# Moving reads and waits in a one-core hybrid attention step: paired read-backs, splits at the change of token group, other tiles for turned outputs, and x rows by GpSimd

## The chip, the cores and the metric

The kernel runs on one core of a Trainium2 chip. The metric is the device time in microseconds (us) of one execution; the number that counts is the median of the runs. Beside the timed runs there is one profiled execution, from which all views of the profile come.

## What is computed

One layer of a streaming encoder: an input projection, two kinds of attention (stick-breaking and retention, 8 heads each, head width 128), a gate, and an output projection. There are 1024 prompt frames and 128 sample frames (8 streams of 16), and 1024 cached frames for each stream. Cut to what matters here:

```python
h = rms_norm(x, norm_pre)
q_sb, k_sb, v_sb, gate_sb, q_r, k_r, v_r, gate_r = split(h @ w_in)    # 2048 -> 8 x 1024
q_r, k_r = rope(q_r), rope(k_r) * HEAD_DIM ** -0.5

def stick_breaking_block(q, k, v):            # a block of 128 queries, keys up to it
    z = q @ k.T * HEAD_DIM ** -0.5
    log_keep = where(strict, log_sigmoid(-z), 0)
    later = reverse_cumsum(log_keep) - log_keep
    return where(strict, exp(log_sigmoid(z) + later), 0) @ v

def retention_chunk(q, k, v, s, log_gamma):   # 64 frames, a state s of 128 x 128
    o = (q @ k.T * gamma ** abs(i - j)) @ v + (q @ s) * decay_read
    s = s * gamma ** n + (k * decay_write).T @ v
    return o, s

y = concat(head_norm(o_sb) * gain * silu(gate_sb), head_norm(o_r) * gain * silu(gate_r))
x = x + rms_norm(y @ w_out, norm_post)        # w_out: 2048 x 2048
```

New keys, values and the retention states are outputs too.

## The kernel before, in words

**Products.** All large products are in 32-bit floats made of two parts. A *split* takes a block and gives a high part, rounded to the matmul's format, by a copy on ScalarE (ACT), and the rest by a subtraction on VectorE (DVE). Each product is then three matmuls (high by high, high by low, low by high). The matmuls run on TensorE (PE).

**Token groups and heads.** The tokens go in two groups: group 0 is prompt tiles 0 to 3 and the sample tile (640 tokens), group 1 prompt tiles 4 to 7 (512 tokens). x lies in SBUF split, in the tiles mh0 to mh3 (high) and ml0 to ml3 (low), each with four of the 16 blocks of 128 columns. For each group there is a loop over 8 heads. A head has a *rows panel* (`project_rows`, matmul at L451), which gives values and gates of the head with weights as the moving operand, 16 steps of k by the tiles of the group by three matmuls, and *projections* (`project`, `products`, L394) for the retention's keys and queries and the stick-breaking's queries and keys, with x as the moving operand. The last head of group 0 takes two of them side by side (`project_pair`). The results leave PSUM by `rope` (two copies on ACT at L495 and L496, three operations on DVE at L497, L498 and L499) or by a multiplication on DVE (L470). The accumulators have four PSUM banks in two rings, acc0 and acc1; a panel of the next head needs banks that ropes must have read.

**Jobs.** Everything else of a head (attention, outputs, loads for later) is written as generators that are *jobs*. After each product of three matmuls the program calls `tick()`, which lets one due job take a step; the number that a job yields is the number of ticks until it is due again. The tables D_* hold these numbers, in pairs for group 0 and group 1. `drain(job)` ticks without products until a job is done. From this program order a scheduler places the instructions on each engine; `pin` ties an instruction so that it is not placed ahead of the products already written. Each engine then runs its own list in order, and a waiting instruction holds up all behind it. A DMA stands in the list of the engine that issues it: SyncE (SP) for most loads, ACT for most stores, GpSimd (POOL) for some of both.

**Transposes through DRAM.** Rows are turned by a store (`turn_out`, L642), a read-back in 32-blocks (`turn_in`, L651) and a transpose on DVE: L747 for the stick-breaking weights of a step (tiles kb, or kp and be), L874 for those of the sample, L1028 for the retention's keys (into rkn), and L722 for a branch's finished output. In `Out.finish` that transpose (L722) goes into a tile that is free by then, rk for the retention and kT for the stick-breaking, is multiplied by the gains (L723), and is stored to DRAM (s_y) for the output projection. The last attention jobs of group 0 run on in the first head of group 1; rk is then also the tile into which that head's `rope` of the keys goes.

**The start.** The x columns are split as they come, for two projections. Then comes the first rows panel. Its jobs (`squares`, L534 for the load, L542 for the operation on ACT) read the rows of x again, in 18 pieces of 512 KB, for the sums of squares of the pre-norm. The panel's weights wrn are loaded at L442, by the same queue, SP.

**The change of token group.** `load_moving` reads the 16 blocks of x of group 1 (tile mr, three buffers, L264) and splits them (L172, L173) in the order of k: 12 of its steps are taken inside `project_pair`, two ahead of each of the six chunks after the first pair (`WQ // 2 if loads and w else 0`), and four in the first four steps of the first rows panel of group 1.

**The output projection.** It is done with seven products of half-size blocks (1 to 7) in place of eight, with sums of blocks made ahead and held in DRAM (s_s for left operands, s_b for weights). A left operand, 8 blocks of 128 x 256, is read back from s_y or s_s by `left()` and split into resident tiles. It keeps two blocks loaded ahead (three buffers mr in group 0; three ahead and four buffers yr in group 1), and before each split the load of a further block is issued; `left_sample` does the same for the sample tile (128 x 128). There are 14 such operands and two of the sample. Weights come through wr (five buffers) by SP as well (L1219) and are split (L167, L168); the matmuls stand at L1202, L1205 and L1206.

## Time and profile before

| | us |
|---|---|
| runs | 2277.29, 2277.5, 2275.72 |
| median | 2277.29 |
| the profiled execution, its own time | 2273.69 |
| its span, first to last instruction | 2271.9 |
| PE busy | 2225.6 (98%) |
| DVE busy | 1264.8 (56%) |
| ACT busy | 922.7 (41%) |
| POOL busy | 421.7 (19%) |
| mean granted clock of PE | 0.994 |

So 1.8 us lie around the span, and the profiled execution is 3.6 us shorter than the median. A row of the timeline has the start, the duration, the engine, the line and the operation with its output and inputs; in brackets stands how long the engine was idle before it, and what ended that idle time. SPq is the queue of DMA issues on SP: the duration there is the time over which the group was issued, and a long one means that the queue stood in between. In the list of waits a row has the waiting engine and line, what released it, the total in us, how often, and the longest. In the windows the columns are the stretch, its length, the busy time of PE, PEld (weight loads), DVE, ACT and POOL with the number of instructions in brackets, the granted clock of PE as a share of full speed, and the DMA engines' busy share and GB/s.

### The profile page before, as it was taken

Reading aid. Unit: us, or ns where it says so; the run is one execution under the profiler, and the core shown is the slowest. Engines: PE = TensorE matmul, PEld = TensorE weight load, DVE = VectorE, ACT = ScalarE, POOL = GpSimd, SP = SyncE. Lnnn points to the kernel's source line nnn. Section 1 sums busy time; section 2 is a strip of 40 time slices with the busy share of each in tenths; the row PEclk is TensorE's granted clock in tenths of the full one; section 3 lists DMA queues with packets and bytes.
Section 4 is the critical chain, followed back from the end, with each engine's and each line's share of the span. In section 5 each row is a group of like instructions: output and inputs, shape, how many; then the busy total and the mean of one; then the engine's idle time right before and its main releaser. Section 6 shows DMA issues by size and latency. Waiting matters only on the chain.

```text
span 2271.9 us, 34748 instructions
## 1 busy us (share of the span) xinstructions
PE 2225.6 (98%) x12002; PEld 1887.4 (83%) x12002; DVE 1264.8 (56%) x2688; ACT 922.7 (41%) x2000; POOL 421.7 (19%) x706
## 2 busy tenths in 40 slices
PE   8999999999999999999999999999999999999998
PEld 7888889798888979797778888888888787778886
DVE  5335445453544445355556666656666657656667
ACT  6423333333333332334333343443433435545563
POOL 0022131322212231221212111120212113000020
PEclk9999999999999999999999999999999999999999
DMA  8567565576656656667767777888788777765785
GB/s 293 175 193 199 180 190 181 176 197 199 193 182 176 206 174 194 185 187 271 204 171 221 241 231 228 234 235 236 234 243 220 216 215 194 236 217 162 215 224 169
DMA packets 383986, 471.25 MB, mean 207 GB/s; under 512 B 121409, under 2 KB 238657, under 8 KB 383297
## 3 DMA queue, kind: packets, MB, share of 16 engines
q1 hardware_dynamic: 256304, 300.41, 44.5%
q0 software_dynamic: 33840, 86.28, 14.1%
q10 hardware_dynamic: 93664, 82.33, 11.6%
q8 instruction: 94, 1.54, 0.3%
q14 instruction: 84, 0.68, 0.1%
HBM read 367.97 MB, written 110.36 MB: 211 GB/s over the span
## 4 chain that ended last, share of the span: by engine, by line
PE 82%; DMA 7%; issue 4%; DVE 4%; ACT 2%; POOL 0%; SPq 0%; DVEq 0%; ACTq 0%; POOLq 0%
PE accm L451 32%; PE acc L394 26%; PE a L1205 5%; PE a L1206 5%; PE a L1202 5%; PE pa L784 2%; PE z L757 2%; PE pd L885 1%; PE zc L824 1%; DMA ro<-s_rk 1%; DMA s_rk<-rk 1%; DMA mr<-x_cols 1%; ACT wh L167 1%; DMA wr<-w_cols 1%; PE rs L906 1%
## 5 line engine op out<-in xcount | busy, mean ns | idle before, releaser
L451 PE MATMUL accm<-whn,mh 128*128 128x512 f32 x1152 | 453.1, 394 | 5.5 <-DVE rq L497 3.7
L451 PE MATMUL accm<-wln,mh 128*128 128x512 f32 x1152 | 453.3, 394 | 1.9 <-DVE wln L168 1.9
L394 PE MATMUL acc<-mh,wh 128*128 128x256 f32 (+2 forms) x1536 | 444.4, 340 | 10.9 <-ACT wh L167 7.1
L451 PE MATMUL accm<-whn,ml 128*128 128x512 f32 x1152 | 453.6, 394 | 0.0
L394 PE MATMUL acc<-ml,wh 128*128 128x256 f32 (+2 forms) x1536 | 445.8, 341 | 0.0
L394 PE MATMUL acc<-mh,wl 128*128 128x256 f32 (+2 forms) x1536 | 445.4, 341 | 0.0
L167 ACT ACTIVATE wh<-wr 128x512 fp32r<-128x512 f32 x408 | 256.7, 631 | 463.2 <-PE acc L394 201.8
L168 DVE TENSOR_TENSOR wl<-wr,wh 128x512 fp32r<-128x512 f32 x408 | 279.2, 687 | 272.4 <-ACT wh L167 258.7
L168 DVE TENSOR_TENSOR wln<-wrn,whn 128x512 fp32r<-128x512 f32 x256 | 175.1, 688 | 296.2 <-ACT whn L167 289.9
L167 ACT ACTIVATE whn<-wrn 128x512 fp32r<-128x512 f32 x256 | 160.9, 632 | 400.2 <-PE accm L451 260.1
L394 PEld LDWEIGHTS acc<-mh,wh 128*128 128x128 f32 x1536 | 284.5, 189 | 30.3 <-ACT wh L167 7.8
L394 PEld LDWEIGHTS acc<-mh,wl 128*128 128x128 f32 x1536 | 282.3, 189 | 25.4 <-issue 6.2
L394 PEld LDWEIGHTS acc<-ml,wh 128*128 128x128 f32 x1536 | 281.7, 189 | 20.6 <-issue 1.7
L451 PEld LDWEIGHTS accm<-whn,mh 128*128 128x128 f32 x1152 | 217.3, 189 | 50.8 <-DVE rq L497 4.7
L451 PEld LDWEIGHTS accm<-wln,mh 128*128 128x128 f32 x1152 | 217.4, 189 | 46.8 <-DVE wln L168 3.5
L451 PEld LDWEIGHTS accm<-whn,ml 128*128 128x128 f32 x1152 | 217.4, 189 | 43.5 <-issue 0.8
L651 POOL DMA_DIRECT2D be<-s_be x128 | 94.1, 742 | 145.1 <-DMA s_be<-be 121.1
L687 DVE TENSOR_TENSOR_SCAN kp<-kp 128x1152 f32<-128x1152 f32 (+4 forms) x40 | 82.7, 2068 | 55.2 <-POOL kp L682 27.9
L1202 PE MATMUL a<-wh,mh 128*128 128x512 f32 x240 | 94.1, 392 | 1.7 <-ACT mh L1262 1.7
L1205 PE MATMUL a<-wl,mh 128*128 128x512 f32 x240 | 93.7, 390 | 1.0 <-DVE wl L168 1.0
L1206 PE MATMUL a<-wh,ml 128*128 128x512 f32 x240 | 93.9, 391 | 0.0
L809 POOL DMA_DIRECT2D kcT<-cache_k x64 | 34.6, 544 | 298.9 <-PE acc L394 123.8
(283 smaller groups left out, 2964.8 us busy)
## 6 DMA issues: line engine op xcount, KB each, us to landing
wr<-w_cols SPq DMA_DIRECT2D x256, 256.0 KB, 4.4
wrn<-w_rows SPq DMA_DIRECT2D x256, 256.0 KB, 3.7
kcT<-cache_k POOLq DMA_DIRECT2D x64, 512.0 KB, 5.0
vc<-cache_v SPq DMA_DIRECT2D x64, 512.0 KB, 5.3
wr<-s_b SPq DMA_DIRECT2D x80, 256.0 KB, 3.8
wr<-w_out SPq DMA_DIRECT2D x80, 256.0 KB, 3.8
br<-w_out SPq DMA_DIRECT2D x64, 256.0 KB, 4.4
s_b<-br ACTq DMA_DIRECT2D x32, 512.0 KB, 5.4
```

The source lines that it names most:

```text
L167: nc.scalar.activation(hi, src, AF.Copy),
L168: nc.vector.tensor_tensor(lo, src, hi.bitcast(F32), ALU.subtract),
L394: last = nc.tensor.matmul(a[:, :m], lhs[:, j, :], rhs[w][:, j, o : o + m], start=(w == 0 and j == 0 and n == 0), stop=(w == KT // WQ - 1 a ...
L451: anchor[0] = nc.tensor.matmul(banks[t], lhs[q][:, j, ts], rhs, start=(k == 0 and n == 0), stop=(k == KT - 1 and n == 2),)
L651: q.dma_start(raw[32 * i : 32 * i + 32, :].rearrange("p (k a) -> p k a", a=32), s[:, :, 32 * i : 32 * i + 32].rearrange("k (j b) a -> b (k ...
L687: nc.vector.tensor_tensor_scan(rev, rev, rev, 1.0, ALU.mult, ALU.bypass)
L757: nc.tensor.matmul(z[:, :c], q2[a][:, i * P : (i + 1) * P], k2[b][:, s : s + c], start=(m == 0), stop=(m == 2),)
L784: nc.tensor.matmul(po[:, :P], at[:, j, :], rest["vn"][j], start=(j == 0), stop=(j == t))
L809: ld = nc.gpsimd.dma_start(kc, cache_k[h, m // 4, m % 4])
L1202: ins = nc.tensor.matmul(a, hi[k][:, ts], wh, start=first, stop=False)
L1205: nc.tensor.matmul(a, hi[k][:, ts], wl, start=False, stop=False)
L1206: anchor[0] = nc.tensor.matmul(a, lo[k][:, ts], wh, start=False, stop=last)
```

## The change

- The rows of x for the sums of squares (xt) are issued by GpSimd, not SyncE.
- The x splits of group 1: inside `project_pair` the steps per chunk are given by `LOADS = 0, 2, 1, 1` (two columns each, so 8 in all); 8 more stand in the first rows panel, at each k but every fourth. Loads and splits are pinned.
- `Out.finish` of the retention transposes into rkn, not rk; that of the stick-breaking in group 1 into the tile be of step 2, not kT.
- `overlap()` adds `D_LATE = 8` ticks, for jobs of group 0 that run on in group 1, ahead of steps that read turned rows. In group 1 D_RK, the wait between a read-back of the keys and its transpose, goes from 18 to 22 ticks.
- `left()` loads blocks in pairs to a buffer of two, as many pairs as there are buffers (three in mr, two in yr), waits D_LEFT = 18 ticks (9 for operands made by `both`), and then splits; the load of a further pair stands behind the second split of a pair. `left_sample` loads all 8 blocks into two buffers of four, waits 18 or 9 ticks, and splits.

No matmul, split, rope or transpose is added or taken away.

```diff
-D_RK = (36, 18)
+D_LATE = 8
+D_RK = (36, 22)
+LOADS = 0, 2, 1, 1
+D_LEFT = 18
...
+    def overlap():
+        return D_LATE if group[0] > phase[0] else 0
...
         def load(k):
             r = wp.tile([P, n], F32, name="mr", tag="mr", bufs=MR)
-            nc.sync.dma_start(r, src(k))
+            pin(nc.sync.dma_start(r, src(k)))
...
-    def left(gi, n, hi, lo, bufs, tag, deep):
+    def left(gi, n, hi, lo, bufs, tag, deep, wait):
...
-        for h in range(deep - 1):
-            load(h)
-        yield D_OP
+        for pair in range(deep):
+            load(pair)
+        yield wait
         for h in range(HT):
-            if h + deep - 1 < HT:
-                load(h + deep - 1)
-            r = raw.pop(0)
-            pin(*split(hi[h], lo[h], r))
+            pin(*split(hi[h], lo[h], raw.pop(0)))
+            if h % 2 and h // 2 + deep < HT // 2:
+                load(h // 2 + deep)
             yield D_OP
...
-                for _ in range(WQ // 2 if loads and w else 0):
+                for _ in range(LOADS[w] if loads else 0):
                     next(loads, None)
...
-            if loads and q == 0:
+            if loads and k % 4 != 3:
                 next(loads, None)
...
-                    nc.sync.dma_start(xt, x_rows(t)[:, c * HALF : (c + 1) * HALF])
+                    nc.gpsimd.dma_start(xt, x_rows(t)[:, c * HALF : (c + 1) * HALF])
...
-                    yield D_TB[phase[0]]
+                    yield D_TB[phase[0]] + overlap()
...
-                        yield D_TR[phase[0]]
+                        yield D_TR[phase[0]] + overlap()
...
-                yield D_TI[phase[0]] // 2
+                yield D_TI[phase[0]] // 2 + overlap()
...
-            yield from out.finish(1, gi, h, 0, rk, s_y[gi][H + h])
+            yield from out.finish(1, gi, h, 0, rkn.rearrange("p k d -> p (k d)"), s_y[gi][H + h])
...
-            yield from out.finish(0, gi, h, 0, kT, s_y[gi][h][:, :NB_TOK])
+            yield from out.finish(0, gi, h, 0, rows[2][1] if gi else kT, s_y[gi][h][:, :NB_TOK])
...
-                made.append(left(g, n, *mine[g, n], *((rp, "yr", 4) if g else (wp, "mr", MR))))
+                made.append(left(g, n, *mine[g, n], *((rp, "yr", 2) if g else (wp, "mr", MR)), D_LEFT // 2))
...
-        ready = [Job(left_sample(1, *mine["s", 1], fp, "ys", 4), 24)]
+        ready = [Job(left_sample(1, *mine["s", 1], fp, "ys", 2, D_LEFT // 2), 24)]
```

The lines of the changed kernel are a few higher than those of before: L495 to L499 are now L501 to L505, L167 and L168 are L170 and L171, L172 is L176, L722 and L723 are L728 and L729, L747 is L753, L874 is L881, L989 and L1007 are L996 and L1014.

How the instructions stand at three places. First ACT at the change of token group. mh is the high part of x (from mr), whn a weight split of the coming rows panel, and the two accumulators are the retention's queries of the last head of group 0, whose rope begins with sw. Before:

```order
L167 ACTIVATE whn<-wrn 128x512
L172 ACTIVATE mh_10431<-mr,pre 128x512
L167 ACTIVATE whn<-wrn 128x512
L172 ACTIVATE mh_10511<-mr,pre 128x512 x3
L167 ACTIVATE whn<-wrn 128x512
L495 ACTIVATE sw<-acc_10263 64x256
L496 ACTIVATE sw<-acc_10263 64x256
L172 ACTIVATE mh_10511<-mr,pre 128x512
L495 ACTIVATE sw<-acc_10264 64x384
L496 ACTIVATE sw<-acc_10264 64x384
```

And with the change:

```order
L170 ACTIVATE whn<-wrn 128x512
L176 ACTIVATE mh_10431<-mr,pre 128x512
L170 ACTIVATE whn<-wrn 128x512
L176 ACTIVATE mh_10431<-mr,pre 128x512
L170 ACTIVATE whn<-wrn 128x512
L176 ACTIVATE mh_10431<-mr,pre 128x512
L501 ACTIVATE sw<-acc_10263 64x256
L502 ACTIVATE sw<-acc_10263 64x256
L501 ACTIVATE sw<-acc_10264 64x384
L502 ACTIVATE sw<-acc_10264 64x384
```

The splits of the third x tile no longer stand ahead of the ropes and between them: eight x splits in all stand ahead now, where there were eleven, and one between.

Second, DVE in the first head of group 1, where attention of group 0's last head runs on: the transpose of the weights kb of a step, the sample's retention (ro, st) and the rope of the new keys (rk, sw). Before:

```order
L168 TENSOR_TENSOR wl<-wr,wh 128x512
L747 STREAM_TRANSPOSE kb<-kb 128x384
L168 TENSOR_TENSOR wl<-wr,wh 128x512
L989 SCALAR_TENSOR_TENSOR ro<-pa,dec,ro 128x128
L1007 SCALAR_TENSOR_TENSOR st<-st,pSs_11261 128x256
L989 SCALAR_TENSOR_TENSOR ro<-pa,dec,ro 128x128
L1007 SCALAR_TENSOR_TENSOR st<-st,pSs_11262 128x256
L498 TENSOR_TENSOR sw<-sw,sinT 128x512
L1007 SCALAR_TENSOR_TENSOR st<-st,pa 128x256
```

With the change:

```order
L996 SCALAR_TENSOR_TENSOR ro<-pa,dec,ro 128x128
L1014 SCALAR_TENSOR_TENSOR st<-st,pSs_11226 128x256
L996 SCALAR_TENSOR_TENSOR ro<-pa,dec,ro 128x128
L1014 SCALAR_TENSOR_TENSOR st<-st,pSs_11227 128x256
L503 TENSOR_TENSOR rk<-acc_11113,cosT 128x512
L1014 SCALAR_TENSOR_TENSOR st<-st,pa 128x256
L881 STREAM_TRANSPOSE kp<-be 128x1152
L1014 SCALAR_TENSOR_TENSOR st<-st,pSs_11240 128x256
L793 COPY so<-pa 128x128
L187 TENSOR_SCALAR ov<-ssq_10041 128x5
L753 STREAM_TRANSPOSE kb<-kb 128x384
```

The transpose of kb stands behind the sample's retention and behind the first read of the keys' bank, where it stood ahead of both.

Third, DVE some 25 us later: the transpose of the retention's finished output (ro), the same for the sample (do), and the ropes. Before:

```order
L168 TENSOR_TENSOR wl<-wr,wh 128x512 x2
L722 STREAM_TRANSPOSE rk<-ro 128x640
L723 TENSOR_SCALAR ro<-rk,gains 128x640
L497 TENSOR_TENSOR rk<-acc_11120,cosT 128x512
L722 STREAM_TRANSPOSE doT<-do 128x128
L499 TENSOR_TENSOR rk<-rk,sw 128x512
```

With the change:

```order
L171 TENSOR_TENSOR wl<-wr,wh 128x512 x2
L503 TENSOR_TENSOR rq<-acc_11353,cosT 128x512
L504 TENSOR_TENSOR sw<-sw,sinT 128x512
L505 TENSOR_TENSOR rq<-rq,sw 128x512
L728 STREAM_TRANSPOSE rkn<-ro 128x640
L915 TENSOR_TENSOR sc<-rs,dT 128x128
L729 TENSOR_SCALAR ro<-rkn,gains 128x640
```

The keys' rope has left this place (it stands in the piece above, some 40 rows ahead), and the queries' rope now stands ahead of the transpose.

More of the change, by code (lines that the diff above doesn't have):

```diff
@@ L202, in tile_hybrid_step @@
     phase = [0]
+    group = [0]
     anchor = [None]
@@ L316, in sums, with load, left_sample @@
             yield pace[2]
[L318 removed]
+    def left(gi, n, hi, lo, bufs, tag, deep, wait):
         src = LEFT[n]
         raw = []
[L322 to L332 removed]
+        def load(pair):
+            r = bufs.tile([P, 2, 256], F32, name=tag, tag=tag, bufs=deep)
+            for i in range(2):
+                h = 2 * pair + i
+                if src[0] == "y":
+                    rows = s_y[gi][src[1] * H + h][:, src[2] * 256 : src[2] * 256 + 256]
+                else:
+                    rows = s_s[gi][h][:, src[1], :]
+                pin(nc.sync.dma_start(r[:, i], rows))
+                raw.append(r[:, i])
+        for pair in range(deep):
+            load(pair)
+        yield wait
         for h in range(HT):
[L334 to L337 removed]
+            pin(*split(hi[h], lo[h], raw.pop(0)))
+            if h % 2 and h // 2 + deep < HT // 2:
+                load(h // 2 + deep)
             yield D_OP
[L340 removed]
+    def left_sample(kk, hi, lo, bufs, tag, deep, wait):
         raw = []
[L343 to L350 removed]
+        for part in range(2):
+            r = bufs.tile([P, HT // 2, P], F32, name=tag, tag=tag, bufs=deep)
+            for i in range(HT // 2):
+                pin(nc.sync.dma_start(r[:, i], s_y[0][kk * H + part * HT // 2 + i][:, 4 * P : 5 * P]))
+                raw.append(r[:, i])
+        yield wait
         for h in range(HT):
[L352 to L353 removed]
             pin(*split(hi[h], lo[h], raw.pop(0)))
@@ L789, in stick_breaking @@
                 yield D_AV[phase[0]]
+            return rows
         waiting = []
@@ L1046, in sb_branch @@
             yield D_NAT[phase[0]]
-            yield from stick_breaking(g, h, out, q2, k2, rest)
+            rows = yield from stick_breaking(g, h, out, q2, k2, rest)
             store_rows(tiles, values[gi, h][:, :, 0, :], v_prompt, v_sample, h)
@@ L1073, in first_left @@
             mine[0, 5] = kept(0)
-            return left(0, 5, *mine[0, 5], wp, "mr", MR)
+            return left(0, 5, *mine[0, 5], wp, "mr", MR, D_LEFT)
         ret_job = sb_job = sub = loads = None
@@ L1083, in tile_hybrid_step @@
                 load_rope(gi)
-            phase[0] = gi
+            phase[0] = group[0] = gi
             for h in range(H):
@@ L1107, in ret_last @@
                     rest = first_left()
+                    next(rest)
                     ret_queries(project(g, mov, col(4, h), rest))
```

33 lines of the change are left out of this document (9 added, 24 removed).

## The prediction, made before the changed kernel had run

> **What bounds the kernel now.** I read the page's first part, then the list of what PE waited for, then windows cut where the granted clock changes.
>
> ```profile
> span 2271.9 us, 34748 instructions
> PE 2225.6 (98%) x12002; PEld 1887.4 (83%) x12002; DVE 1264.8 (56%) x2688; ACT 922.7 (41%) x2000; POOL 421.7 (19%) x706
> ```
>
> PE is the bound: it idles for 2271.9 - 2225.6 = 46.3 us. The change adds and removes no matmul, so it can gain only out of these 46.3 us, and out of the time in which PE runs at a lower clock. Where the idle time lies:
>
> ```profile
> PE acc L394 <- ACT wh L167: 7.1, 1, 7.1
> PE pa L784 <- DVE kp L747: 6.0, 6, 2.3
> PE accm L451 <- DVE rq L497: 3.7, 2, 2.2
> PE acc L394 <- DVE rk L497: 3.5, 1, 3.5
> PE pSs L1003 <- DVE st L1007: 2.6, 1, 2.6
> PE a L1202 <- ACT wh L167: 2.0, 2, 1.1
> PE a L1205 <- DVE wl L168: 1.7, 4, 1.0
> PE a L1202 <- ACT mh L1262: 1.7, 1, 1.7
> PE accm L451 <- ACT whn L167: 1.6, 1, 1.6
> ```
>
> The first row is the start of the kernel, which nothing here touches. The others are single stalls of 1 to 3.5 us, each with its own place, and most are a wait behind something else on DVE or ACT. The windows show what follows such a stall (the granted clock stands after POOL's busy time):
>
> ```profile
> 64.93:68.34 3.41, 3.31 (x8) 2.66 (x9) 2.08 (x4) 3.23 (x6) 0.00 (x0) 0.50 0.70 219
> 1044.55:1051.38 6.83, 5.04 (x12) 3.65 (x13) 5.17 (x12) 5.21 (x9) 0.00 (x0) 0.50 0.79 241
> 1119.65:1123.06 3.41, 3.41 (x16) 2.81 (x18) 1.85 (x5) 1.64 (x4) 0.00 (x0) 0.50 0.28 92
> 1140.13:1146.96 6.83, 6.01 (x14) 4.84 (x15) 3.15 (x7) 1.82 (x3) 2.75 (x5) 0.50 0.55 172
> 1766.20:1772.00 5.80, 5.61 (x33) 4.96 (x34) 2.42 (x11) 2.41 (x5) 0.00 (x0) 1.00 0.72 221
> 2020.00:2261.65 241.65, 241.65 (x1067) 199.74 (x1065) 155.62 (x327) 123.54 (x281) 19.78 (x23) 1.00 0.66 188
> ```
>
> Four times the clock is 0.50, for 3.41 or 6.83 us. Half of that is lost: 1.7, 3.4, 1.7 and 3.4 us, 10.2 us in all. The fifth row shows a stall (2.33 us, quoted below) with no such loss. The last row shows the output projection's second part without any idle time: 241.65 us for 1067 matmuls, 0.227 us each, which is the pitch of a 512-wide matmul.
>
> The Trainium skill (TensorE: Matmul & The Clock Gate, Part 1: The HAM clock gate) says that the clock is halved after an idle window of some 3.4 us that runs freely, and is restored after as long a busy one. The lengths 3.41 and 6.83 us agree with one window and two. That idle spans of under 3 us were enough here disagrees, if the window must be idle throughout.
>
> **The change part by part.**
>
> *First rows panel.* SP first, the queue of loads:
>
> ```profile
> 27.11 12.00 SPq L442 DMA_DIRECT2D wrn<-w_rows  x6
> 50.84 5.45 SPq L534 DMA_DIRECT2D xt<-x_prompt  x4
> 56.38 1.87 SPq L442 DMA_DIRECT2D wrn<-w_rows  x4
> ```
>
> then ACT and PE:
>
> ```profile
> 63.62 1.97 ACT L167 ACTIVATE whn<-wrn 128x512 fp32r<-128x512 f32 x3 [6.00 <-DMA wrn<-w_rows]
> ```
>
> ```profile
> 64.31 0.49 PE L451 MATMUL accm<-whn,mh 128*128 128x512 f32 x1 [1.63 <-ACT whn L167]
> ```
>
> The x rows xt go ahead of the panel's weights wrn in SP's list, which stands at them until a buffer is free; so weights are issued again only at 56.38, ACT waits 6.00 us for them and PE 1.63, and the clock drops. With xt in POOL's list SP has only weights here. What has to hide the new place: POOL has nothing else to issue at this time (0.00 busy in the window at 64.93), and the only loads behind xt there are the cached keys (kcT), which come with the attention jobs after the panel. ACT's sums of squares still stand between weight splits, and each waits for its xt. Both queues move blocks of this size in the same time (size in KB, then us from issue to landing):
>
> ```profile
> kcT<-cache_k POOLq DMA_DIRECT2D x64, 512.0 KB, 5.0
> xt<-x_prompt SPq DMA_DIRECT2D x16, 512.0 KB, 5.1
> ```
>
> A panel step of five tiles takes 15 x 0.227 = 3.4 us, 16 of them 54 us, against 18 loads in four buffers, 18 / 4 x 5 = 23 us. So it is hidden twice over. Gain: 1.63 + 1.7 = **3.3 us**.
>
> *The change of token group.* ACT, then PE:
>
> ```profile
> 1042.35 0.72 ACT L172 ACTIVATE mh<-mr,pre 128x512 fp32r<-128x512 f32 x1 [1.21 <-DMA mr<-x_cols]
> 1043.61 0.38 ACT L495 ACTIVATE sw<-acc 64x256 f32<-64x256 f32 x1
> ```
>
> ```profile
> 1039.26 0.45 PE L394 MATMUL acc<-mh,wl 128*128 128x256 f32 x2
> 1039.55 0.45 PE L394 MATMUL acc<-mh,wh 128*128 128x256 f32 x2
> ```
>
> ```profile
> 1044.89 0.80 PE L451 MATMUL accm<-whn,mh 128*128 128x512 f32 x1 [2.24 <-DVE rq L497]
> 1047.98 0.79 PE L451 MATMUL accm<-whn,mh 128*128 128x512 f32 x1 [1.45 <-DVE rq L497]
> ```
>
> The ropes of the queries start at 1043.61 because x splits that wait for their DMA stand ahead on ACT. But the queries' accumulators are complete a whole chunk before PE's last product of the pair: 12 products of two pieces at 0.29 us (1039.55 - 1039.26), 3.5 us. With three splits fewer ahead, the ropes can run beside PE's last chunk, and end with it. Bounds: if ACT is still late, only the pieces between the ropes fall, the second wait, 1.45 us; if it is in time, both waits and the clock, 2.24 + 1.45 + 3.4 = 7.1 us. I take **6.0**, near the upper end, since the order has the ropes directly behind a split whose x was due some microseconds sooner. The price is eight x splits of 0.72 us in the panel rather than four; a panel step of four tiles is 12 x 0.227 = 2.7 us there, so they fit beside it.
>
> *Transpose of kb.* DVE, then PE:
>
> ```profile
> 1116.13 0.58 DVE L747 STREAM_TRANSPOSE kb<-kb 128x384 f32<-128x384 f32 x1 [5.03 <-DMA kb<-s_be]
> ```
>
> ```profile
> 1117.92 0.59 PE L1003 MATMUL pSs<-vv,rkn 32*128 32x128 f32 x3 [2.57 <-DVE st L1007]
> ```
>
> DVE stands 5.03 us for a read-back, with the sample's retention and the keys' rope queued behind. D_LATE puts the transpose behind these. The read-back landed by 1116.1 and ten operations of DVE now go first, so little wait is left. Gain 2.57 + 1.7 = **4.3 us**.
>
> *Output transposed into another tile.* DVE, then PE:
>
> ```profile
> 1138.55 0.84 DVE L722 STREAM_TRANSPOSE rk<-ro 128x640 f32<-128x640 f32 x1
> ```
>
> ```profile
> 1140.11 0.69 DVE L497 TENSOR_TENSOR rk<-acc,cosT 128x512 f32<-128x512 f32 x1
> ```
>
> ```profile
> 1140.95 0.77 PE L394 MATMUL acc<-mh,wh 128*128 128x512 f32 x1 [3.49 <-DVE rk L497]
> ```
>
> The rope of the new keys writes rk, and so can't go before the old output has passed through rk. With rkn the rope stands some 40 rows ahead. A read-back that comes late would now hold up only scores (sc) and weight splits. Gain 3.49 + 3.4 = **6.9 us**, the largest term.
>
> *D_RK 22.* DVE, then PE:
>
> ```profile
> 1762.83 0.71 DVE L1028 STREAM_TRANSPOSE rkn<-ro 128x512 f32<-128x512 f32 x1 [2.39 <-DMA ro<-s_rk]
> ```
>
> ```profile
> 1766.39 0.82 PE L784 MATMUL pa<-vo,kp 128*128 128x128 f32 x5 [2.33 <-DVE kp L747]
> ```
>
> DVE waits 2.39 us for the keys' read-back, and the transpose that PE needs stands behind. Four ticks of three matmuls are 4 x 0.68 = 2.7 us, more than that wait. Gain **2.3 us** here. The other five waits of this kind (6.0 - 2.3 = 3.7 us) I leave as they are.
>
> *Left operands.* ACT's waits, then SP ahead of an operand:
>
> ```profile
> ACT mh L167 <- DMA mr<-s_y: 19.3, 17, 4.8
> ACT mh L167 <- DMA mr<-s_s: 11.8, 12, 2.8
> ```
>
> ```profile
> 1995.99 1.38 SPq L325 DMA_DIRECT2D mr<-s_y  x3
> ```
>
> Loads are asked for two blocks ahead, too late, and ACT stands 31.1 us for them in all. PE pays for that in the three rows of `a` above: 2.0 + 1.7 + 1.7 = 5.4 us, of which an unknown part is weights that came late by themselves. Six blocks at once and a wait of 9 or 18 ticks end most of ACT's waits. Against it stands that six loads go ahead of weights at a stroke, three more than in the row above, 1.4 us on SP. Gain between 5.4 us and a loss of 1.4; I take **4.0**.
>
> *What comes in their place.* Four of the cleared stalls end at an operation of DVE that still takes its time; I leave 0.69 us (the rope's row at 1140.11) at three of them, 2.1 us, and one drop of the clock, 1.7 us: 3.8 us back.
>
> Sum: 3.3 + 6.0 + 4.3 + 6.9 + 2.3 + 4.0 - 3.8 = **23.0 us**. The profiled execution would be 2273.7 - 23.0 = 2250.7. It is 3.6 us below the median of the runs; against the median of 2277.3 the same gain makes **2254.3 us**, 1.0% faster. No change means within 0.2%, 4.6 us, about what a measurement of this kernel can tell.
>
> By the page's rule on the clock, a leftover wait of under 3.4 us costs no clock; the sum would then be 24.7.
>
> **The rivals.**
>
> *Other waits take over.* Where one wait goes, the next late operation may stand within a microsecond, and an idle time of 1.6 us has cost clock (64.31, above). For it: DVE and ACT are lists in order, and all of them are written anew here. Against: in the three pieces of order what PE waits for stands ahead of anything that waits for a DMA. If the change of group gives only its 1.45, the left operands nothing, and one more clock drop of 3.4 stays, the gain is 23.0 - 4.6 - 4.0 - 3.4 = 11 us: 2266.
>
> *The queue of loads blocks the weights (slower).* In `left()` the load of the last pair stands on SP behind a split, and weights stand behind that load. If the split is late, SP stands, and PE runs out of weights: per operand the 1.4 us of three more loads, and 1.7 for a clock drop, 3.1 us. From eight of the 16 operands on (24.8 us) this eats the whole gain; with ten of them the time is 2254 + 31 = 2285. For it: PE already waits for weight splits (2.0 and 1.7). Against: eight of the 16 operands (products 5 and 3 of group 1, and 6, 7 and 4 of both) are read in 2020 to 2261.65, where PE doesn't wait, and the 9 or 18 ticks let the split find its data landed.
>
> *GpSimd's loads are slow beside DVE.* If xt came late, ACT's squares would hold up weight splits, and the first term, 3.3 us, would be lost: 2257.6. PE needs the fifth weight split, which stands behind the fourth square, at about 37 + 4 x 3.4 = 51 us, so loads would have to take four times their 5.0 us. The Trainium skill (DMA: Bandwidth & Descriptors, SWDGE vs HWDGE vs iDMA) warns of this: GpSimd writes its descriptors into memory that DVE locks in its two-port mode, and SP's loads are immune. The two equal landing times above don't show such a cost.
>
> *The change does nothing.* The scheduler could have restored the old order. The orders before and after differ at all three places, so this leaves only waits that come back through DMAs: within 4.6 us of 2277.
>
> **How the numbers follow.** The forecast (gain of 17 to 31 us): 0.62, of which GpSimd's loads 0.03. Other waits take over: 0.20. Nothing: 0.07. Blocked weights: 0.11. The upper gain is everything at its bound with nothing put back: 3.3 + 7.1 + 4.3 + 6.9 + 2.3 + 5.4 = 29.3, 2248, and a few small waits more; I set the low end at 2245. The high end takes in the second case: 2268. Outside lie nothing and blocked weights, 0.18. Faster 0.82, same 0.07, slower 0.11.
>
> **What would show it.** In the changed kernel's list of PE's waits: no row of accm <- whn, none of acc <- rk of over 1 us, accm <- rq and pSs below 1 us, and the granted clock 1.00 in the windows at 1050, 1120 and 1140 shifted by the gain. ACT's waits for mr from s_y and s_s should fall from 31.1 us to under 10. Wrong would be: new rows of `a` <- wh at 1900 to 2020, clock drops left at the change of group, or PE's busy time not falling by some 8 us.

## The result and the profile after

| | before | after |
|---|---|---|
| median of five runs each, same chip | 2277.29 us | 2255.89 us |
| ratio to before, 95% interval | | 0.9909 [0.9896, 0.9923] |
| profiled execution, its own time | 2273.69 us | 2256.29 us |
| span | 2271.9 us | 2254.4 us |
| PE idle, span less busy | 46.3 us | 34.9 us |
| PE busy | 2225.6 us | 2219.5 us |

The change makes the kernel 0.9% faster. The median falls by 21.4 us and the profiled span by 17.5: the profiled execution of before lay 3.6 us below its median, that of after at it. Of the 17.5 us, 11.4 are less idle time of PE and 6.1 less busy time for the same 12002 matmuls. The first part of the page of after:

```profile
span 2254.4 us, 34741 instructions
PE 2219.5 (98%) x12002; PEld 1884.7 (84%) x12002; DVE 1266.5 (56%) x2688; ACT 922.2 (41%) x2000; POOL 434.6 (19%) x724
```

What PE waited for in after (waiting engine and line, what released it, total in us, times, longest):

```profile
PE acc L400 <- ACT wh L170: 7.5, 1, 7.5
PE pa L790 <- DVE kp L753: 3.9, 3, 3.5
PE rs L913 <- DVE rq L505: 2.9, 3, 2.5
PE a L1210 <- ACT wh L170: 1.7, 1, 1.7
PE pS L946 <- DVE rkn L1039: 1.6, 1, 1.6
...
PE accm L457 <- DVE rq L503: 1.0, 1, 1.0
```

All of `accm` <- whn, `acc` <- rk and pSs <- st are gone, and `accm` <- rq is down from 3.7 to 1.0. New are pS <- rkn and one wait of 2.5 us in rs <- rq, of which before had five of at most 0.4. And pa <- kp, six waits before, is now almost all one wait of 3.5. The windows over the three places and over the stretches where the clock now falls, cut at the change of the clock (granted clock behind POOL's busy time):

```profile
34.00:68.00 34.00, 33.26 (x151) 27.54 (x150) 13.72 (x30) 24.01 (x45) 6.88 (x13) 1.00 0.82 280
1030.00:1060.00 30.00, 28.83 (x163) 23.47 (x162) 19.04 (x38) 16.48 (x35) 3.17 (x6) 1.00 0.85 295
1100.00:1150.00 50.00, 48.54 (x294) 36.87 (x293) 33.06 (x87) 18.11 (x47) 14.53 (x23) 1.00 0.69 202
1875.10:1881.93 6.83, 6.07 (x19) 5.28 (x20) 3.94 (x10) 1.20 (x4) 3.40 (x6) 0.50 0.71 185
1927.00:1940.00 13.00, 9.52 (x50) 7.84 (x50) 9.15 (x24) 6.26 (x16) 2.18 (x4) 1.00 0.56 167
1991.14:1994.55 3.41, 3.41 (x9) 2.64 (x8) 2.87 (x7) 2.58 (x7) 0.00 (x0) 0.50 0.94 316
```

The four half-clock stretches of before are gone, 10.2 us of loss. Two new ones cost 3.4 and 1.7 us, both in the stage in which left operands are loaded beside the last attention jobs. What happens there shows first on SP (when, and over how long, the loads of a group were issued):

```profile
1856.32 3.18 SPq L339 DMA_DIRECT2D mr<-s_s  x6
1859.60 1.64 SPq L1227 DMA_DIRECT2D wr<-s_b  x2
1862.17 1.25 SPq L339 DMA_DIRECT2D mr<-s_s  x2
```

then on ACT, DVE and PE:

```profile
1869.40 0.77 ACT L170 ACTIVATE mh<-mr 128x256 fp32r<-128x256 f32 x2 [4.27 <-DMA mr<-s_s]
```

```profile
1869.85 0.43 DVE L171 TENSOR_TENSOR ml<-mr,mh 128x256 fp32r<-128x256 f32 x1 [3.06 <-ACT mh L170]
...
1872.60 0.83 DVE L753 STREAM_TRANSPOSE kp<-be 128x640 f32<-128x640 f32 x1
1873.37 0.65 DVE L503 TENSOR_TENSOR rq<-acc,cosT 128x512 f32<-128x512 f32 x1
```

```profile
1872.14 0.50 PE L1213 MATMUL a<-wl,mh 128*128 128x512 f32 x1 [1.39 <-DVE wl L171]
...
1875.86 0.80 PE L913 MATMUL rs<-rq,rk 128*128 128x128 f32 x2 [2.53 <-DVE rq L505]
```

The fourth pair of an operand (x2) can be issued only when the first pair has been split. ACT then stands 4.27 us for it, DVE 3.06 us for ACT, and behind DVE's half of the split stand a weight split, a transpose and the rope of the queries, for which PE waits 1.39 and 2.53 us. One read-back that is late on ACT so holds up work on DVE that has nothing to do with it.

To see where the time went I took from the timeline when PE starts certain matmuls of its list, counted from its first. Each column is the time between two of them; with the 7 us ahead and the 10 behind they add up to the span. The stages are: A the start and the first rows panel (matmul 0 to 300); B the rest of group 0 (to 6300, at 1031 us in after); C the change of group and the first head after it (to 8000, 1372 us); D the heads after that (to 9800, 1747 us); E the rest, with the output projection. The jobs shift a few matmuls across such a border. All the kernels of this study stand in it, the experiments ahead of their telling:

| kernel | A | B | C | D | E |
|---|---|---|---|---|---|
| before | 59.0 | 968.5 | 355.8 | 378.8 | 492.0 |
| after | 56.5 | 967.4 | 340.7 | 375.4 | 497.1 |
| after, profiled again | 56.9 | 967.4 | 339.6 | 375.8 | 495.2 |
| after, old left operands | 59.0 | 967.5 | 339.4 | 378.4 | 503.0 |
| before, new left operands | 59.1 | 967.5 | 359.6 | 378.3 | 498.7 |
| after, D_RK 18 | 57.6 | 967.5 | 341.0 | 383.2 | 490.0 |
| after, both old tiles | 57.2 | 967.5 | 344.0 | 377.6 | 490.2 |
| after, kT again (rkn kept) | 56.9 | 967.5 | 340.7 | 379.7 | 491.8 |
| the same, D_RK 20 | 56.8 | 967.5 | 341.9 | 381.4 | 498.7 |
| the same, spaced pairs | 57.9 | 967.4 | 339.4 | 377.7 | 490.4 |
| after, spaced pairs | 57.0 | 967.4 | 339.7 | 377.7 | 496.6 |
| after, D_LATE 0 | 58.2 | 967.5 | 340.0 | 376.1 | 494.8 |
| after, old x splits | 57.5 | 967.5 | 346.7 | 374.3 | 498.1 |
| after, xt by SP | 56.8 | 967.4 | 340.7 | 376.9 | 497.0 |

After gains 2.5, 1.1, 15.1 and 3.4 us in A to D, and gives 5.1 back in E. Two profiles of after differ by up to 1.9 us in a stage. Six profiles (after twice, old left operands, kT, spaced pairs twice) have the same order of instructions up to 1757 us, two of them with kT in the place of be, and they spread more: 56.5 to 59.0 us in A, 339.4 to 340.7 in C, 375.4 to 379.7 in D. So the gain in C is clear, and a gain in D isn't shown, since before's 378.8 lies among them. The same holds for A: the 59.0 us of the old left operands hold no stall of over 0.8 us, but the first matmuls run slowly for longer there (28 in the first 6.9 us, 55 in the next 6.3; in before the slow stretch is 3.2 us long). Before's stages come from one profile, 3.6 us below its median; the kernel before with new left operands has the same order through D, and takes 359.6 us in C rather than 355.8.

### The profile page after: what moved, and what is told of

The parts are those of the page before. It is cut to its first block, busy times and chain, and to the rows that moved or that the text cites. A ratio compares the mean times of both kernels' runs of the same rounds, so it can differ in the third digit from the quotient of the medians.

```text
span 2254.4 us, 34741 instructions
## 1 busy us (share of the span) xinstructions
PE 2219.5 (98%) x12002; PEld 1884.7 (84%) x12002; DVE 1266.5 (56%) x2688; ACT 922.2 (41%) x2000; POOL 434.6 (19%) x724
## 3 DMA queue, kind: packets, MB, share of 16 engines
q8 instruction: 94, 1.54, 0.3%
## 4 chain that ended last, share of the span: by engine, by line
PE 86%; DMA 6%; DVE 3%; issue 3%; ACT 1%; POOL 0%; SPq 0%; ACTq 0%; DVEq 0%; POOLq 0%
PE accm L457 33%; PE acc L400 28%; PE a L1214 5%; PE a L1213 5%; PE a L1210 5%; PE z L763 2%; PE pa L790 2%; PE zc L831 1%; DMA wr<-w_out 1%; PE pd L892 1%; DMA xc<-x_cols 1%; PE rs L913 1%; PE pa L931 1%; PE pS L946 1%; DMA wr<-w_cols 1%
## 5 line engine op out<-in xcount | busy, mean ns | idle before, releaser
L170 ACT ACTIVATE wh<-wr 128x512 fp32r<-128x512 f32 x408 | 257.1, 631 | 486.6 <-PE acc L400 207.2
L171 DVE TENSOR_TENSOR wl<-wr,wh 128x512 fp32r<-128x512 f32 x408 | 279.6, 688 | 281.8 <-ACT wh L170 258.2
L171 DVE TENSOR_TENSOR wln<-wrn,whn 128x512 fp32r<-128x512 f32 x256 | 175.3, 688 | 270.7 <-ACT whn L170 268.0
L170 ACT ACTIVATE whn<-wrn 128x512 fp32r<-128x512 f32 x256 | 161.2, 632 | 393.4 <-PE accm L457 258.8
L682 POOL TENSOR_SCALAR_AFFINE_SELECT kp<-kp 128x128 f32<-128x128 f32 x40 | 13.7, 342 | 374.3 <-ACT kp L676 369.2
```

What stands on the lines that cost most here:

```text
L170: nc.scalar.activation(hi, src, AF.Copy),
L171: nc.vector.tensor_tensor(lo, src, hi.bitcast(F32), ALU.subtract),
```

## The experiments

Ratios are to the kernel before on the same chip; after itself stands at 0.9909 [0.9896, 0.9923].

**Old left operands in the changed kernel.** `left()`, `left_sample` and their calls as before, all else as changed.

> The changed kernel, with left() and left_sample() as before (one block to a buffer, no longer wait). Theory: the new read-backs cost time, since the last pair can be loaded only after a whole pair is split; the stalls of PE between 1870 and 1990 us (1.4, 2.5, 0.8, 3.5 and 1.7 us, and 5 us of clock) go back to the 6.6 us of the kernel before, and the time falls from 2255.9 to about 2248. Rival: those stalls come from the other parts of the change (the whole timeline is 15 us earlier there), and the new read-backs gain their 4 us: then this kernel is slower than the changed one, about 2260.

Measured: 2263.09 us, 0.9945 [0.9933, 0.9958], 8 us slower than after. So the rival's direction came, at twice its size: with the other edits in place, the new left operands are worth some 8 us. Stage E is 503.0 us, longer still than after's 497.1. The longest wait of PE in this kernel after its start (lines are three higher here):

```profile
PE rs L916 <- DVE rq L508: 6.4, 4, 4.9
```

The 4.9 us are one wait that ends at 1886 us, and its cause on DVE is the same chain as in after, only longer:

```profile
1877.61 0.86 DVE L171 TENSOR_TENSOR ml<-mr,mh 128x256 fp32r<-128x256 f32 x2 [4.49 <-ACT mh L170]
```

**New left operands in the kernel before.**

```diff
-        for h in range(deep - 1):
-            load(h)
-        yield D_OP
+        for pair in range(deep):
+            load(pair)
+        yield wait
...
```

> The kernel before, with the new left() and left_sample() alone. Theory: about 8 us slower than before, 2285. Rival: about 4 us faster, 2273, as the prediction's term for left operands has it.

Measured: 2281.74 us, 1.0020 [1.0011, 1.0030]: alone, the same edit costs 4.5 us. Its stage E is 6.7 us longer than before's, and one wait makes most of that, on PE and on DVE ahead of it:

```profile
1957.98 1.79 PE L782 MATMUL pa<-vo,kp 128*128 128x128 f32 x8 [4.77 <-DVE kp L745]
```

```profile
1956.01 0.77 DVE L169 TENSOR_TENSOR ml<-mr,mh 128x256 fp32r<-128x256 f32 x2 [2.13 <-ACT mh L168]
1956.69 1.24 DVE L745 STREAM_TRANSPOSE kp<-be 128x1024 f32<-128x1024 f32 x1
```

The transpose for PE stands behind a split of operand blocks whose load (mr from s_s) is late. What the edit is worth depends on which transpose or rope happens to stand behind such a split: it has no price of its own.

**D_RK back to 18.**

```diff
-D_RK = (36, 22)
+D_RK = (36, 18)
```

> The changed kernel with D_RK = 18 in group 1. Theory: the wait at 1540 us for rkn (1.6 us) goes, and the one of 2.3 us that the kernel before had at 1764 comes back: about 2257, within 2 us of the changed kernel. Rival: the other waits of PE for kp (1.2, 0.9 and 0.7 us in the kernel before) went by D_RK too and come back as well: about 2259.

Measured: 2257.45 us, 0.9922 [0.9908, 0.9935], not told apart from after. In stage D this kernel is 7.8 us longer than after (waits of 1.1, 2.0, 0.9 and 2.2 us at 1438, 1641, 1730 and 1749), 3.5 to 7.8 us longer than the six profiles with 22 ticks named above, and in stage E it is 7.1 us shorter than after. So 22 ticks gain in their own stage, and the shifted order loses it again later.

**Both old tiles.**

```diff
-            yield from out.finish(1, gi, h, 0, rkn.rearrange("p k d -> p (k d)"), s_y[gi][H + h])
+            yield from out.finish(1, gi, h, 0, rk, s_y[gi][H + h])
-            yield from out.finish(0, gi, h, 0, rows[2][1] if gi else kT, s_y[gi][h][:, :NB_TOK])
+            yield from out.finish(0, gi, h, 0, kT, s_y[gi][h][:, :NB_TOK])
```

> The changed kernel with finished outputs transposed into rk and kT again. Theory: the rope of the new keys waits for the read-back again at about 1125 us; PE stands about 3.5 us and the clock is halved for one or two windows of 3.41 us: 5 to 7 us slower than the changed kernel, 2261 to 2263. Rival: with the other waits gone the read-back is in time, and the tile makes no difference: 2256.

Measured: 2255.78 us, 0.9915 [0.9901, 0.9928], the same as after. PE's two waits at 1127 and 1133 us:

```profile
1127.04 0.47 PE L400 MATMUL acc<-mh,wh 128*128 128x512 f32 x1 [3.38 <-DVE rk L503]
1133.53 0.71 PE L913 MATMUL rs<-rq,rk 128*128 128x128 f32 x4 [2.81 <-DVE rq L505]
```

```profile
1120.00:1150.00 30.00, 23.81 (x119) 19.13 (x118) 18.94 (x50) 8.72 (x23) 6.99 (x12) 1.00 0.51 143
```

The wait for rk is back, 3.38 us against 3.49 in before, but no half clock follows it (the last section shows why). Stage C is 3.3 us longer than after's, and stage E 6.9 us shorter: what the new tiles gain early is gone again late.

**rkn for the retention, kT for the stick-breaking.** Of the two tile edits, the second is undone.

```diff
-            yield from out.finish(0, gi, h, 0, rows[2][1] if gi else kT, s_y[gi][h][:, :NB_TOK])
+            yield from out.finish(0, gi, h, 0, kT, s_y[gi][h][:, :NB_TOK])
```

> The changed kernel, with the stick-breaking's finished output transposed into kT again and the retention's still into rkn. Up to about 1765 us its order is the changed kernel's, from there on that of the run with both old tiles. Theory: the tile be moves work of the last heads so that PE waits more there (3.5 and 2.5 us and a clock drop in the changed kernel, 1.6 us with both old tiles), while rkn saves the 6 us of PE's waits at 1123 to 1130: 2250, ratio to before 0.9885. Rival: the later stalls differ from run to run and the tile be has no part in them: 2255, ratio 0.991.

Measured: 2253.81 us, 0.9896 [0.9879, 0.9913]. Stage C is after's (340.7) and stage E lies near that of the old tiles (491.8), as it should be if rkn carries the gain and be of step 2 the loss. The ratio is 0.0013 below after's, and the intervals overlap. Some of what stage E gains is lost in D, at 1540 us, where DVE waits for the keys' read-back twice as long as in after, with the same order there:

```profile
1541.56 0.71 DVE L1035 STREAM_TRANSPOSE rkn<-ro 128x512 f32<-128x512 f32 x1 [3.51 <-DMA ro<-s_rk]
```

**The same with D_RK 20.**

```diff
-D_RK = (36, 22)
+D_RK = (36, 20)
```

> The kernel with rkn and kT (the run before of that name), with D_RK = 20 in group 1. In that run and in the changed kernel PE waited 3.3 and 1.6 us at 1540 us for keys whose read-back had not landed after 22 ticks; with 18 ticks it did not wait there, but 0.9 to 2.2 us at five other places of group 1. Theory: such waits come from the time at which the read-back lands, and the ticks only choose the place: 20 ticks give about the same sum, 2252 to 2256, ratio to before 0.9895. Rival: 20 ticks avoid both kinds: 2250, ratio 0.988.

Measured: 2260.26 us, 0.9931 [0.9917, 0.9945], slower than the same kernel with 22 ticks, against both expectations. (18 ticks were run with the tile be alone, and the intervals overlap.) PE waits 10.2 us for kp, nearly all of it in three waits of 2.4, 3.3 and 4.0 us at 1436, 1542 and 1934. With 22 ticks, in the run above, no wait for kp is over 1.8 us, but one of 3.3 us for the keys stands at 1540. So the time is no smooth function of D_RK; why two ticks bring these three together stays open.

**Old x splits at the change of group.** Loads and splits unpinned.

```diff
-LOADS = 0, 2, 1, 1
+LOADS = 0, 2, 2, 2
...
-            if loads and k % 4 != 3:
+            if loads and q == 0:
```

> The changed kernel with the x splits of group 1 as before (12 steps inside the pair of projections, four in the first rows panel, loads and splits not pinned). PE's order is unchanged by this; only ACT, DVE and SP differ. Theory: the ropes of the queries start late again; PE waits 2.2 and 1.4 us at the change of token group and the clock is halved for 6.8 us: 6 us slower than the changed kernel, ratio to before 0.9935. Rival: only the wait between the ropes comes back, 1.4 us, ratio 0.9915.

Measured: 2264.3 us, 0.9946 [0.9931, 0.996], 8 us slower than after; the profile is 6.3 us longer than after's, 6.0 of it in stage C. PE's waits at the place, which half a clock of 6.83 us follows:

```profile
1042.47 0.50 PE L457 MATMUL accm<-whn,mh 128*128 128x512 f32 x1 [2.75 <-DVE rq L503]
1045.57 0.79 PE L457 MATMUL accm<-whn,mh 128*128 128x512 f32 x1 [2.13 <-DVE rq L503]
```

**xt by SP again.**

```diff
-                    nc.gpsimd.dma_start(xt, x_rows(t)[:, c * HALF : (c + 1) * HALF])
+                    nc.sync.dma_start(xt, x_rows(t)[:, c * HALF : (c + 1) * HALF])
```

> The changed kernel with the x rows xt issued by SyncE again. Theory: the panel's weights stand behind them, PE waits 1.6 us at about 62 us and 0.6 us at 38, and the clock is halved for 3.4 us: 3.5 to 4 us slower than the changed kernel, ratio 0.9925. Rival: without the early loads of mr the weights are in time by themselves: ratio 0.991.

Measured: 2258.51 us, 0.9923 [0.9908, 0.9938], not told apart from after. Stage A is 56.8 us, as good as with GpSimd. ACT still waits as long as in before for a weight:

```profile
63.84 1.30 ACT L170 ACTIVATE whn<-wrn 128x512 fp32r<-128x512 f32 x2 [6.14 <-DMA wrn<-w_rows]
```

but PE doesn't wait here. In this kernel the x loads of group 1, pinned, no longer stand in SP's list among the first panel's weights, and one weight split more is done before the wait. The kernel with the old x splits has the other half: xt by GpSimd, the x loads unpinned among the weights, and no such wait either. So each of the two edits removes the stall at 62 us, and the second one adds nothing.

**D_LATE 0.**

```diff
-D_LATE = 8
+D_LATE = 0
```

> The changed kernel with D_LATE = 0. Theory: DVE stands for the read-back of kb ahead of the sample's retention again, PE waits 2.6 us at about 1100 us and the clock is halved for 3.4 us: 4.3 us slower than the changed kernel, ratio 0.993. Rival: the other edits have already moved the transpose, and the eight ticks add nothing: ratio 0.991.

Measured: 2258.07 us, 0.992 [0.9904, 0.9937], not told apart from after. DVE, then PE:

```profile
1107.11 0.58 DVE L753 STREAM_TRANSPOSE kb<-kb 128x384 f32<-128x384 f32 x1 [3.74 <-DMA kb<-s_be]
```

```profile
1108.90 0.59 PE L1010 MATMUL pSs<-vv,rkn 32*128 32x128 f32 x3 [1.28 <-DVE st L1014]
```

The wait for kb is there again, 3.74 us on DVE, yet PE pays 1.28 us, and its clock stays at 1.00. Stage C isn't longer than after's.

**Pairs asked for one at a time, with kT.** On the kernel with rkn and kT:

```diff
         for pair in range(deep):
             load(pair)
-        yield wait
+            yield wait // deep
...
-                    next(rest)
+                    for _ in range(MR):
+                        next(rest)
```

> The kernel with rkn and kT, with left() loading its pairs one by one, the wait of 18 or 9 ticks shared out between them, in place of all pairs at a stroke. Theory: at about 1986 us weights stand on SP behind six loads of 131 KB, and PE waits 1.7 to 2.8 us for the weight split (2.7 in the run with rkn and kT); with weights let in between, this wait falls below 1 us and that at 1911 us (1.8) as well: 2 to 4 us faster, about 2251, ratio to before 0.988 to 0.9885. Rival: the weights are late because their buffers come free late, and the order of the loads changes nothing: 2254, ratio 0.9896.

Measured: 2251.07 us, 0.9889 [0.9873, 0.9905], the lowest of all, though its interval overlaps after's and that with kT. It aims at this place of after, on SP and ACT:

```profile
1979.04 3.45 SPq L339 DMA_DIRECT2D mr<-s_y  x6
1983.64 2.05 SPq L1227 DMA_DIRECT2D wr<-w_out  x3
```

```profile
1988.95 1.91 ACT L170 ACTIVATE wh<-wr 128x512 fp32r<-128x512 f32 x3 [2.55 <-DMA wr<-w_out]
```

Six loads ahead of three weights: ACT waits 2.55 us for a weight, and PE 1.67 us in after, 2.67 in the kernel with kT. With the pairs spaced, SP issues two, then four, with weights between, and PE waits 0.85 us:

```profile
1974.53 0.90 SPq L339 DMA_DIRECT2D mr<-s_y  x2
1975.54 1.00 SPq L1228 DMA_DIRECT2D wr<-w_out  x2
1977.57 3.06 SPq L339 DMA_DIRECT2D mr<-s_y  x4
1980.73 3.70 SPq L1228 DMA_DIRECT2D wr<-w_out  x3
```

```profile
1986.37 0.49 PE L1211 MATMUL a<-wh,ah 128*128 128x512 f32 x1 [0.85 <-ACT wh L170]
```

The wait at 1911, which was to fall below 1 us as well, only goes from 1.78 to 1.54 us.

**Pairs asked for one at a time, with the changed kernel's tiles.** The same edit on after.

> The changed kernel with one edit: left() asks for its pairs one at a time, with the wait shared among them, so no six loads stand together ahead of weights; both tile edits stay as changed. Theory (the burst of loads is what the late stalls come from): the stalls of PE on weights at 1988 and on the weight splits at 1871 to 1873 (1.67, 1.39 and 2.53 us in the changed kernel) fall below 1 us each, the one at 1928 below 2, no half clock there; 3 to 8 us less than the changed kernel, ratio to before about 0.9875, and below that of the changed kernel run beside it. Rival (the tile be of step 2 causes them, and spacing alone does nothing): the stalls at 1873 and 1928 stay above 2 us and the ratio stays within 0.0015 of the changed kernel's.

Measured: 2257.98 us, 0.9916 [0.9898, 0.9934], the same as after. PE's waits in it:

```profile
1874.02 0.50 PE L1214 MATMUL a<-wl,mh 128*128 128x512 f32 x1 [1.55 <-DVE wl L171]
1877.75 0.80 PE L913 MATMUL rs<-rq,rk 128*128 128x128 f32 x2 [2.51 <-DVE rq L505]
```

The stall at 1988 is gone (no wait of over 0.5 us there), as the theory has it. Those at 1874 and 1877 stay to within 0.2 us, as the rival has it. So the burst of six loads causes the one at 1988 and not these. The wait for rq is there, 2.51 to 2.53 us long, in all six profiles with be of step 2, D_RK 22 and the new left operands; in the four of the changed kernel with kT it is 0.21 us at most at that place. After and the run with kT differ in this tile alone, so the tile is its cause in that company.

**After once more**, beside it.

> The changed kernel once more, unedited, beside the spaced one on the same chip. If the stalls at read-backs vary from run to run as the experiments with an equal order suggest, the stall at 1540 is anywhere from 0.5 to 3.3 us and the half-clock stretches stand elsewhere or are gone, while the ratio to before stays at 0.991 within 0.0013. If they are a fixed property of the order, the stalls at 1540, 1873 and 1928 are again 1.58, 2.53 and 3.48 us within 0.3.

Measured: 2255.91 us, 0.9908 [0.9893, 0.9922], after's ratio again.

```profile
1875.38 0.80 PE L913 MATMUL rs<-rq,rk 128*128 128x128 f32 x2 [2.52 <-DVE rq L505]
```

Neither expectation holds whole. The wait for rq is a fixed property of the order (2.53 us in after, 2.51 with the pairs spaced). Others move from run to run: the one at 1540 from 1.58 to 1.98, at 1928 from 3.48 to 2.04, at 1988 from 1.67 to 1.95.

## Why the prediction was right, and where its steps were not

The predicted time, 2254.3 us, is 1.6 us below the measured median, and the stalls at the early places are gone as forecast, though not each by the edit that was to remove it. That the sum is so near is in part luck. In the profiles the stages A to D gained 22.1 us, where the terms for them make 22.8; E lost 5.1, where the left operands were to gain 4.0. So the profiled execution took 2256.3 us and not 2250.7. The median gained 3.9 us more than the profile, for the most part because the profiled execution of before lay 3.6 us below its median.

Of the three signs of being wrong, the clock drops at the change of group didn't come; of `a` <- wh one row of 1.67 us stands at 1988, where before had 1.07 and 0.94; and PE's busy time fell by 6.1 us, not 8.

*First rows panel (3.3).* Measured 2.5 us in A and 1.1 in B, 3.6 in all, with the clock at 1.00; A spreads as much between profiles. The reason was half the story: the move of xt to GpSimd is enough, but so are the pinned x loads (xt by SP). xt landed in 6.3 us (median) by GpSimd in after, in 5.1 by SP in before and 6.0 in the kernel with xt by SP; nothing of that reaches PE.

*The change of group (6.0).* Right. One wait of 0.97 us is left, and undoing the edit costs 6.0 us in its stage and 8 us in the whole. ACT and PE in after:

```profile
1036.55 0.72 ACT L176 ACTIVATE mh<-mr,pre 128x512 fp32r<-128x512 f32 x1 [2.30 <-DMA mr<-x_cols]
1037.29 0.38 ACT L501 ACTIVATE sw<-acc 64x256 f32<-64x256 f32 x1
```

```profile
1041.05 0.50 PE L457 MATMUL accm<-whn,mh 128*128 128x512 f32 x1 [0.97 <-DVE rq L503]
```

The queries' rope still stands behind one late x split, by 2.30 us; it needed only to be one and not three.

*Transpose of kb (4.3).* In after the wait of 2.57 us and its clock drop are gone, but D_LATE isn't what they hang on: without it PE waits 1.28 us and the clock holds. At most 1.3 us of the 4.3 are D_LATE's.

*Output tile (6.9).* Both tile edits together are worth 3.3 us in stage C, all of it rkn's (stage C with rkn and kT is after's). The term counted a clock drop of 3.4 us with a wait of 3.49; the wait came back at 3.38, the drop didn't, and whether one follows such a wait is in part luck (last section). And the term had no price for the second tile edit, which shares its bullet in the change: in stage E it costs 3 to 6 us (497.1 and 495.2 against 491.8; with the pairs spaced, 496.6 against 490.4).

These three terms were 17.2 us together, and stage C gained 15.1. Undone one at a time they give 6.0, 3.3 and nothing. The 5.8 us between that and 15.1 (more against the 359.6 of before's order in its other profile) belong to no single edit; no run takes two of them out together, so how they share it stays open.

*D_RK 22 (2.3).* Stage D gained 3.4 against before, within the spread of D, and loses 3.5 to 7.8 if 18 is put back: the direction is shown, the size isn't. I left the other waits for kp as they were; of before's waits at 1453, 1744 and 1840 (1.17, 0.85 and 0.68 us) none of over 0.4 is left. The price that I didn't count is stage E, 7.1 us shorter with 18, and a new wait for the keys' read-back, 1.58 us on PE, which isn't there with 18. The row of that wait on DVE names another DMA that ended last; with kT, above, it names the read-back itself:

```profile
1539.50 0.71 DVE L1035 STREAM_TRANSPOSE rkn<-ro 128x512 f32<-128x512 f32 x1 [1.83 <-DMA out<-x_prompt]
```

*Left operands (4.0).* This is the step that failed. "Six blocks at once and a wait of 9 or 18 ticks end most of ACT's waits" was meant to gain 4.0; stage E lost 5.1. That loss isn't this edit's by itself: with the old left operands in the changed kernel E is longer still (503.0), while with D_RK 18 or with kT, each put back alone, it is 490.0 and 491.8, near before's 492.0. So the loss belongs to these edits together, and no term priced what they do to E. ACT's waits for mr did fall:

```profile
ACT mh L170 <- DMA mr<-s_s: 10.1, 5, 4.3
...
ACT mh L170 <- DMA mr<-s_y: 3.3, 2, 2.7
```

13.4 us from 31.1, a little above the 10 that I named. But the seven waits that are left are longer, 1.9 us in the mean, where before had 29 of 1.1 us; and some of them stand where DVE's list has a rope or a transpose for PE behind them. My upper bound was taken from the `a` rows of PE alone, while the harm comes by pa <- kp and rs <- rq. Nor is there one right number for the term: it is +8 us in the changed kernel (old left operands) and -4.5 in the kernel before.

*What comes in their place (-3.8).* Too small, and in the wrong place: 1.7 us were left for the clock, and 3.4 + 1.7 were lost, all in the stage of the left operands. At the cleared stalls 0.97 us of waiting is left, of 2.1 allowed.

*The rivals.* Other waits do take over, late and not at the places cleared. The queue of loads does block weights once, at 1988, 1.67 us and a clock drop of 1.7, 3.4 us together beside the 3.1 priced for an operand; it happens at one operand, not at eight.

## What to carry to other kernels

Where several engines run fixed lists, price an edit in the company it will have: the same edit was worth 8 us in one order and cost 4.5 in another, and two edits that clear the same stall gain once. A wait that is moved off one list should be followed to the second engine that depends on it (here ACT's split, then DVE's, then whatever stands behind that on DVE): ACT's waits for these loads fell from 31.1 to 13.4 us here, and PE still stood 1.39, 2.53 and 3.48 us behind what was left. Compare stages between fixed instructions, not whole times: an early gain and a late loss of 7 us each look like an edit that does nothing. And give a drop of the clock behind a stall a chance, not a fixed price.

## What the runs showed of the hardware that was not expected

The length of a stall alone doesn't decide whether PE's clock falls. In after 3.48 us at 1928 are followed by a clock of 1.00 (window at 1927 above), as are 3.38 and 2.81 us in the kernel with the old tiles (its window at 1120); but 1.39 and 2.53 us close together at 1872 to 1876 come with 6.83 us at half clock, and 1.67 us at 1988 with 3.41, which begin 1.5 us after the wait has ended.

The traces show what does. In each of the fourteen profiles all changes of the clock lie whole multiples of 3.413 us apart, and where this grid lies against the kernel's start differs from profile to profile. I cut each profile along its own grid, from 20 to 2235 us, and took PE's idle time in each window at full clock. The 36 windows with half clock behind them hold 1.50 to 3.39 us of idle time, 30 of them more than 1.90. The others hold 1.90 us at most; 8982 hold less than 1.50, 17 lie between. So by these counts a window of which about half is idle costs the clock, wherever in the window the idle time lies; the ends of matmuls are modelled, so the edge isn't sharper than that. Three windows of after:

```profile
1871.68:1875.09 3.41, 1.19 (x4) 0.67 (x4) 3.41 (x6) 3.10 (x7) 0.63 (x1) 1.00 0.63 180
1926.29:1929.71 3.42, 1.83 (x9) 1.17 (x7) 1.70 (x5) 2.23 (x6) 0.00 (x0) 1.00 0.98 268
1929.71:1933.12 3.41, 1.51 (x13) 1.51 (x14) 3.22 (x7) 1.85 (x5) 0.00 (x0) 1.00 0.51 167
```

In the first PE is busy for 1.19 us, and half clock follows at 1875.09. The grid cuts the wait of 3.48 us at 1928 into 1.58 and 1.90, and none follows. With the old tiles it cuts the wait for rk into 1.70 and 1.68. The window that holds the 1.67 us at 1988 ends at 1991.14, where the clock falls. Since the grid lies elsewhere in each profile, the drop behind a wait of 2 to 3.5 us is in part luck; none of the runs moves a wait against the grid by itself. The Trainium skill (TensorE: Matmul & The Clock Gate, Part 1: The HAM clock gate) speaks of windows of about 3.4 us that run freely; the lengths of the drops and the grid agree with it. The prediction's reading, that a leftover wait of under 3.4 us costs no clock, doesn't hold here: the 1.67 us at 1988 were enough.

Waits for read-backs through DRAM are not a constant of the order: PE's wait at 1540 was 1.58, 1.98, 1.91, 2.66, 3.26 and 2.33 us in the six profiles with the same order up to there (the last two with kT), and 0.54 us with the old x splits, whose order is another at the change of group. The wait for rq repeated to 0.02 us in six: 1.2 us after the wait for wl has ended, PE stands again, and between wl and rq lie only operations of DVE.
